# A hybrid decoder step on one core: the order of loads at a stage's start, squares at other tiles, and banks for the last transposes

## The chip, the cores and the metric

The kernel runs on one core of a Trainium2 chip. TensorE does the matrix products, VectorE and ScalarE the work on single elements, GpSimd some of it and the issue of part of the DMAs, and SyncE issues the rest of the DMAs. All run at once and wait for each other by semaphores. The metric is the device time of one execution in microseconds (us), the median of several runs.

## The reference

One layer of a decoder for 512 prompt tokens and 8 single sample tokens, all in float32. D is 2048.

```python
m = mixer(rmsnorm(x, norm_mix_g), ...)   # proj = xn @ w_in; bg, cg, hin, q, k, v, og, glr = split(proj)
#   ya = bg * causal_conv3(cg * hin)                               1024 channels
#   o  = gated linear attention over q, k, v (4 heads), normalised
#   yb = o * silu(og)                                              1024 channels
#   m  = concat(ya, yb) @ w_out
x = x + m
f = conv_ffn(rmsnorm(x, norm_ffn_g), ...)  # h = silu(causal_conv3(u) + b) * v; f = h @ w_down
x = x + f
return rmsnorm(x, final_norm_g), and the new convolution and attention states
```

## The kernel before, in words

Activations lie with channels on the 128 partitions and the 520 tokens along the free axis. Each float32 product is made of three products of parts: an operand is split into a high part (a rounded copy, made by ScalarE, line 111, 123 or 1223) and a low part (the rest, made by VectorE, line 112, 124 or 1227).

**Start (lines 283 to 535).** x comes in rows of tokens and is transposed on TensorE, tile by tile of 128 channels (`x_copy`, copied out of PSUM by VectorE at line 385), scaled and split (`x_split`, low part at line 127), and also stored to memory by a DMA that GpSimd issues (line 389). The loop over k from 0 to 15 multiplies tile k at once by the first weights (line 480, helper line 140), copies up to tile k + 3 and splits tile k + 2. Beside that the squares of x are summed for the norm: ScalarE squares the channels of chunks 1 to 3, and for chunk 0, kept as four tiles of 128x512, GpSimd squares one whole tile in place in each of the iterations k = 8 to 11 (line 492); VectorE sums them at k = 14 and 15. Each of TensorE, VectorE, ScalarE and GpSimd keeps the order in which the program text is written here (`InOrder`, lines 58 to 90).

**Attention and convolution (to line 1122).** The mixer's first projections, the attention of four heads, which leaves its output in memory (`o_d`, line 1093, issued by GpSimd for the last head), and the sums and differences of blocks of x (`mixer_sums`), which go to memory as `mt_d`.

**Mix groups (from line 1640).** The other projections are made with seven products in place of eight: blocks of weights and blocks of x are added first, and each "form" of x is a sum. Form 5 is used by the second product of a group, form 4 by the third, form 6 and 7 later. Form 5, 4 and 6 have three tiles each to fetch from `mt_d` and form 7 four (`load_sum`, line 1599: a DMA on SyncE's queue now, and a function that splits the tile later). Ahead of the loop over `order` (line 1699) the program finishes two tiles of the gate `og`: `y8` and `y9`, each the product of a plain projection, are evacuated (`evac`, line 544), passed through silu, and multiplied by the attention's output `on[0]`, `on[1]`, which is loaded from `o_d` (line 1652). `prepare(i)` (line 1208) makes the high and low part of product i's weights and the next sum of weights. `load_rest(0)` (line 1206) loads a weight block into a buffer that VectorE must have left. From line 823 to line 1799 all five queues, SyncE's and GpSimd's too, keep the order of the text. So in SyncE's queue the loads from `o_d` stand first, then the weight block, then the sums; and on VectorE the product of `y8` with `on[0]` (line 1664, helper 1291) stands between the evacuation of `y8` and the splits.

**The end (lines 1822 to 1903).** The last products of the output are made for two halves of the tokens (`half`): first 264 tokens in three tiles, then 256 in two. For each of 16 tiles m of channels, TensorE multiplies, VectorE adds what was summed before (line 642), and `rows(m)` transposes the result back to rows of tokens (line 1836), one iteration later. Four tiles m share one PSUM bank per tile of tokens. ScalarE squares and sums a bank (line 1846); the last bank in two pieces, columns 0 to 383 after m = 14 and the rest after m = 15. Then come the norm's factor (lines 1880 to 1884, `newton`) and the scaling of four quarters: the first and second by ScalarE (line 1896), the last by VectorE straight out of PSUM (line 1890), the third by VectorE (line 1894), each followed by the store of its result on SyncE's queue (line 1898). Here the framework chooses the order on the engines.

Of the kernel before, what the change touches and what calls it, by code (L numbers as in the profile page):

```python
# [9 lines left out]
F32 = mybir.dt.float32  # L10
# [3 lines left out]
ALU = mybir.AluOpType  # L14
# [3 lines left out]
P = 128  # L18
# [19 lines left out]
def trunk_kernel(  # L38
# [53 lines left out]
    def tmp():  # L92
        return tp.tile([P, T], F32, tag="t", name="t")
# [189 lines left out]
    with ExitStack() as es:  # L283
# [193 lines left out]
        for k in range(KD):  # L477
            c, t = k // 4, k % 4
            for i, ps in enumerate(first if k else ()):
                span(ps, ws[c], xa, k, 4 * (c - i), 1, KD)  # L480
            while upto < min(k + (3 if k < 3 else 4), KD):
                x_copy(upto)
                upto += 1
            if k + 2 < KD:
                x_split(k + 2)
            if t == 0 and c < 2:
                raws.append(load_w(c + 2))
                load_x(xc[c + 2], (c + 2) * 512)
            if t == 1 and c < 3:
                ws.append(parts(raws[c + 1], 8))  # L490
            if 8 <= k < 12:
                nc.gpsimd.tensor_tensor(xc[0][t], xc[0][t], xc[0][t], op=ALU.mult)
# [797 lines left out]
    def mult(out, x, y):  # L1290
        nc.vector.tensor_tensor(out, x, y, op=ALU.mult)
# [355 lines left out]
    w11, first = raw_tile(lambda m, k: mix_source(0, m, k), 1)  # L1647
    nc.sync.dma_start(*first)
    early = {(1, 1): w11, **second_half(lambda m, k: mix_source(0, m, k))}
    on = [tmp()[:, :T] for _ in range(2)]  # L1650
    for j, x in enumerate(on):
        nc.sync.dma_start(x, o_d[j])
    ps = new_mm()
    span(ps, ws_og[0], xa, 0, 0, 8, KD)
    ws = [parts(*raws[0])]
# [166 lines left out]
    def half(b, tiles):  # L1822
        t0, n = PARTS[b]
        fin = fp.tile([P, len(tiles), D], F32, name=f"y{b}")
        sums = fp.tile([P, 3, 5], F32, tag="sums", name="sums", bufs=2)
        nc.vector.memset(sums, 1.0)
        pt, outs = [None], {}

        def rows(m):


            if m % 4 == 0:
                pt[0] = [bank() for _ in tiles]
            out = outs.pop(m)
            for i, (u0, un) in enumerate(tiles):
                nc.tensor.transpose(  # L1836
                    pt[0][i][:un, (m % 4) * P : (m % 4 + 1) * P],
                    out[:, u0 - t0 : u0 - t0 + un], idn,
                )
            if m % 4 == 3 or m == KD - 2:  # L1840
                b = m // 4
                c0, c1 = (0, 512) if b < 3 else ((0, 384), (384, 512))[m % 2]
                for i, (u0, un) in enumerate(tiles):
                    junk = tmp()
                    n = b + (c0 > 0)
                    nc.scalar.activation(
                        junk[:un, c0:c1], pt[0][i][:un, c0:c1], AF.Square,
                        accum_out=sums[:un, i, n : n + 1],
                    )
                    if b < 3:  # L1850
                        f = fin[:un, i, b * 512 : (b + 1) * 512]
                        mult(f, pt[0][i][:un, :], gf[:un, b * 512 : (b + 1) * 512])

        for m2 in range(0, KD, 2):
            wh, wl = piece(w_down, NF - CH, CH, m2 * P, 2 * P)
            for m in (m2, m2 + 1):
                ps = mm_bank()
                co = (m - m2) * P
                for i in range(CH):
                    mm3(  # L1860
                        [ps[:, :n]], (wh[:, i, co : co + P], wl[:, i, co : co + P]),
                        hs[b][i], i == 0, i == CH - 1,
                    )
                    if i == 1:
                        tick()
                outs[m] = tmp()
                q = 2 * (m % 4 // 2)
                for u0, u1 in ((t0, min(t0 + n, HT)), (HT, t0 + n)):
                    if u0 < u1:
                        a = two(acc[m // 4, q + (u0 >= HT)])[:, m % 2, u0 % HT :][:, : u1 - u0]  # L1870
                        add(outs[m][:, u0 - t0 : u1 - t0], ps[:, u0 - t0 : u1 - t0], a)
                if m:
                    rows(m - 1)

        def finish():
# [4 lines left out]
            nc.vector.reduce_sum(var, sums, axis=mybir.AxisListType.X)  # L1880
            nc.scalar.activation(rs, var, AF.Ln, scale=1.0 / D, bias=eps_t)
            nc.vector.tensor_scalar(vv, var, 1.0 / D, EPS, op0=ALU.mult, op1=ALU.add)
            nc.scalar.activation(rs, rs, AF.Exp, scale=-0.5)
            newton(rs, vv, tn, nc.vector)
            for b in (0, 3, 1, 2):
                for i, (u0, un) in enumerate(tiles):
                    f = fin[:un, i, b * 512 : (b + 1) * 512]
                    r = rs[:un, i : i + 1]
                    if b == 3:
                        nc.vector.scalar_tensor_tensor(  # L1890
                            f, pt[0][i][:un, :], r, gf[:un, b * 512 :], op0=ALU.mult, op1=ALU.mult
                        )
# [5 lines left out]
                    nc.sync.dma_start(dst[:, b * 512 : (b + 1) * 512], f)  # L1898

        return finish  # L1900
# [42 lines left out]
```

## Time and profile before

| what | us |
|---|---|
| median of 3 runs | 2163.0 (2161.82 to 2163.73) |
| the profiled execution | 2160.99 |
| its span, first to last instruction | 2159.3 |
| TensorE busy / VectorE / ScalarE / GpSimd | 2134.2 / 1734.5 / 1111.6 / 439.7 |
| stretch 0 to 56 (start), TensorE busy | 53.47 |
| stretch 431 to 477.5 (start of the mix groups), TensorE busy | 43.69 of 46.5 |
| stretch 692 to 840 (output projection and what follows), TensorE busy | 142.12 of 148 |
| stretch 2145.1 to 2159.3 (the end), TensorE busy | 2.56 of 14.2 |

A row of the timeline gives the start in us from the span's start, the duration in us, the engine (PE is TensorE, DVE VectorE, ACT ScalarE, POOL GpSimd, SPq SyncE's queue), the line, the operation, and output<-inputs by the program's names; x2 says that two in a row are merged. A bracket gives the idle time of the engine ahead of the instruction and what ended it. In a row of the grouped waits stand the engine, who was waited for, the time in all, how often, and the longest.

### The profile page before, as it was taken

To read this page: it belongs to the slowest core of one execution; us is meant where nothing else is said; L and a number is where in the kernel's file an instruction comes from. 1 tells how busy PE (TensorE), PEld (TensorE's weight loads), DVE (VectorE), ACT (ScalarE), POOL (GpSimd) and SP (SyncE) were. 2 spreads that over 40 slices of the span, in tenths; PEclk is the share of its full clock that TensorE was granted. 3 is DMA by queue.
4 is the path that set the end of the run, shared out by engine and by line. 5 is a ranking of instruction groups with operands and counts; after the bars stand their busy time and mean duration, and the time that the engine had idled before them with its cause. 6 is when DMAs were issued, how large, how long until landed. Compare 5 with 4: busy or idle time off the path is not lost.

```text
span 2159.3 us, 43820 instructions
## 1 busy us (share of the span) xinstructions
PE 2134.2 (99%) x17749; PEld 2112.2 (98%) x17749; DVE 1734.5 (80%) x2302; ACT 1111.6 (51%) x1631; POOL 439.7 (20%) x625
## 2 busy tenths in 40 slices
PE   9999999999999999999999999999999999999997
PEld 8999999999999999999999999999999999999997
DVE  7347465588888898998998998998998778888886
ACT  6435435355544586555555555555555554444445
POOL 5113131211243421121221131122121300200000
PEclk9999999999999999999999999999999999999999
DMA  8545464388888996667676676676677866994734
GB/s 258 145 131 157 121 190 121 93 247 215 206 259 248 297 268 181 181 183 189 166 191 176 167 195 179 163 198 178 169 193 192 287 206 161 274 291 134 225 108 158
DMA packets 467163, 415.51 MB, mean 192 GB/s; under 512 B 21641, under 2 KB 426393, under 8 KB 466817
## 3 DMA queue, kind: packets, MB, share of 16 engines
q1 hardware_dynamic: 424081, 289.71, 47.0%
q0 software_dynamic: 42832, 122.93, 21.7%
q8 instruction: 139, 2.28, 0.4%
q14 instruction: 63, 0.52, 0.1%
q10 hardware_dynamic: 48, 0.07, 0.0%
HBM read 299.45 MB, written 80.31 MB: 176 GB/s over the span
## 4 chain that ended last, share of the span: by engine, by line
PE 90%; DMA 3%; DVE 3%; ACT 1%; issue 1%; POOL 0%; SPq 0%; ACTq 0%; DVEq 0%; POOLq 0%
PE mm L1247 34%; PE mm L140 14%; PE ms L1247 14%; PE x L1490 9%; PE y L1490 9%; PE f L1490 3%; PE e L1490 3%; PE ms L982 1%; DMA form<-g_d 1%; DMA g_d<-t 1%; DMA yl<-t_d 0%; DMA yl<-mt_d 0%; PE ms L1836 0%; DMA raw<-raw 0%; PE ms L968 0%
## 5 line engine op out<-in xcount | busy, mean ns | idle before, releaser
L1247 PE MATMUL mm<-yl,hi 128*128 128x260 f32 x1696 | 476.6, 281 | 3.4 <-DVE yl L124 3.4
L1247 PE MATMUL mm<-yh,hi 128*128 128x260 f32 x1696 | 476.1, 281 | 2.4 <-ACT ms L1257 1.2
L1247 PE MATMUL mm<-yh,lo 128*128 128x260 f32 x1696 | 475.2, 280 | 0.8 <-DVE lo L1227 0.8
L1223 ACT ACTIVATE hi<-raw 128x1024 fp32r<-128x1024 f32 x324 | 342.0, 1056 | 233.8 <-issue 89.4
L1227 DVE TENSOR_TENSOR lo<-raw,hi 128x1024 fp32r<-128x1024 f32 x324 | 395.4, 1220 | 36.0 <-ACT hi L1223 33.0
L1227 DVE TENSOR_TENSOR lo<-s,hi 128x1024 fp32r<-128x1024 f32 x243 | 298.4, 1228 | 124.9 <-ACT hi L1223 124.9
L1223 ACT ACTIVATE hi<-s 128x1024 fp32r<-128x1024 f32 x243 | 257.4, 1059 | 220.7 <-PE ms L1247 93.6
L1247 PEld LDWEIGHTS mm<-yl,hi 128*128 128x128 f32 x1696 | 319.8, 189 | 4.0 <-DVE yl L124 4.0
L1247 PEld LDWEIGHTS mm<-yh,hi 128*128 128x128 f32 x1696 | 319.5, 188 | 3.0 <-ACT ms L1257 1.4
L1247 PEld LDWEIGHTS mm<-yh,lo 128*128 128x128 f32 x1696 | 319.2, 188 | 1.2 <-DVE lo L1227 1.2
L1247 PE MATMUL ms<-b,hi 128*128 128x260 f32 x1408 | 266.3, 280 | 0.0
L1247 PEld LDWEIGHTS ms<-b,hi 128*128 128x128 f32 x1408 | 223.2, 189 | 0.0
L1490 PE MATMUL x<-form,hi 128*128 128x260 f32 x1120 | 211.5, 281 | 0.1
L1490 PE MATMUL y<-form,hi 128*128 128x260 f32 x1120 | 211.3, 281 | 0.0
L1168 DVE TENSOR_TENSOR s<-s,raw 128x1024 f32<-128x1024 f32 x162 | 197.9, 1221 | 2.8
L1247 PE MATMUL ms<-b,lo 128*128 128x260 f32 x704 | 198.1, 281 | 0.0
L1490 PEld LDWEIGHTS x<-form,hi 128*128 128x128 f32 x1120 | 176.4, 188 | 0.7 <-issue 0.5
L1490 PEld LDWEIGHTS y<-form,hi 128*128 128x128 f32 x1120 | 176.4, 188 | 0.3
L112 DVE TENSOR_TENSOR lo<-raw,hi 128x1024 fp32r<-128x1024 f32 x76 | 94.9, 1253 | 78.0 <-ACT hi L111 77.9
L1490 PE MATMUL x<-form,lo 128*128 128x260 f32 x560 | 156.7, 280 | 0.1
L1490 PE MATMUL y<-form,lo 128*128 128x260 f32 x560 | 156.7, 280 | 0.0
L1247 PEld LDWEIGHTS ms<-b,lo 128*128 128x128 f32 x704 | 132.4, 188 | 0.0
(382 smaller groups left out, 5066.2 us busy)
## 6 DMA issues: line engine op xcount, KB each, us to landing
raw<-in_w_up_dram SPq DMA_DIRECT2D x176, 512.0 KB, 4.6
raw<-in_w_down_dram SPq DMA_DIRECT2D x96, 512.0 KB, 4.7
raw<-in_w_in_dram SPq DMA_DIRECT2D x92, 512.0 KB, 4.5
form<-f_d SPq DMA_DIRECT2D x126, 260.0 KB, 6.2
raw<-raw POOLq DMA_DIRECT2D x56, 512.0 KB, 5.9
f_d<-t POOLq DMA_DIRECT2D x80, 260.0 KB, 5.6
raw<-in_w_out_dram SPq DMA_DIRECT2D x32, 512.0 KB, 13.8
form<-g_d POOLq DMA_DIRECT2D x42, 260.0 KB, 7.6
```

What stands on the lines that cost most here:

```text
L112: nc.vector.tensor_tensor(lo, raw, hi.bitcast(F32), op=ALU.subtract)
L140: nc.tensor.matmul(o, w, xx, start=first and i == 0, stop=last and i == 2)
L982: nc.tensor.matmul(pb[:, c * 64 : (c + 1) * 64], L[:, c, :], rhs[:, c], start=True, stop=True,)
L1168: return lambda: nc.vector.tensor_tensor(out, x, y, op=ALU.add)
L1223: nc.scalar.activation(his[i], src, AF.Copy)
L1227: nc.vector.tensor_tensor(los[i], src, his[i].bitcast(F32), op=ALU.subtract)
L1247: nc.tensor.matmul(st["bank"][b], w[:, k, :], x, start=b not in st["used"] and k == 0 and j == 0, stop=k == 7 and j == 2, skip_group_check ...
L1490: nc.tensor.matmul(ps[:, m, :], w[:, k, m * P : (m + 1) * P], x, start=b not in st["used"] and k == 0 and j == 0, stop=k == 3 and j == 2, ...
```

## The change

There are three edits.

First, at the start of the mix groups: the three loads of the sums of form 5 are issued where the two loads of the attention's output stood, ahead of the weight block. Behind the weight block come the sums of form 4, then the attention's output, then the sums of form 6. The product of `y8` with `on[0]` moves on VectorE from behind the silu to behind the evacuation of `y9`.

Second, in the start: GpSimd squares the four tiles of chunk 0 in iterations 6, 7, 10 and 11 in place of 8, 9, 10 and 11.

Third, at the end: in the half with two tiles of tokens, the transposes of the last tile (m = 15) go to two banks of their own. In both halves the last 512 columns are squared in three pieces (0 to 255 after m = 13, 256 to 383 after m = 14, 384 to 511 after m = 15), with a column more in the table of sums, and where the banks differ the scaling of the last quarter is two instructions.

```diff
-            if 8 <= k < 12:
-                nc.gpsimd.tensor_tensor(xc[0][t], xc[0][t], xc[0][t], op=ALU.mult)
+            if k in (6, 7, 10, 11):
+                x = xc[0][(6, 7, 10, 11).index(k)]
+                nc.gpsimd.tensor_tensor(x, x, x, op=ALU.mult)
...
-    on = [tmp()[:, :T] for _ in range(2)]
-    for j, x in enumerate(on):
-        nc.sync.dma_start(x, o_d[j])
+    put = [load_sum(mt_d, 5, g) for g in range(1, 4)]
     ps = new_mm()
     span(ps, ws_og[0], xa, 0, 0, 8, KD)
     ws = [parts(*raws[0])]
...
     begin(0)
     load_rest(0)
-    put = [load_sum(mt_d, f, g) for f in (5, 4, 6) for g in range(1, 4)]
+    put += [load_sum(mt_d, 4, g) for g in range(1, 4)]
+    on = [tmp()[:, :T] for _ in range(2)]
+    for j, x in enumerate(on):
+        nc.sync.dma_start(x, o_d[j])
+    put += [load_sum(mt_d, 6, g) for g in range(1, 4)]
     y8, y9 = zpad[0][:, 2 : 2 + T], tmp()[:, :T]
     evac(ps, y8)
     nc.scalar.activation(y8, y8, AF.Silu)
-    mult(y8, y8, on[0])
...
     evac(ps, y9)
+    mult(y8, y8, on[0])
     mult(R2, R, R)
...
-        sums = fp.tile([P, 3, 5], F32, tag="sums", name="sums", bufs=2)
+        sums = fp.tile([P, 3, 6], F32, tag="sums", name="sums", bufs=2)
...
+            if m == KD - 1:
+                pt[1] = [bank() for _ in tiles] if len(tiles) < 3 else pt[0]
+            pb = pt[m == KD - 1]
...
-            if m % 4 == 3 or m == KD - 2:
+            if m % 4 == 3 or m > KD - 4:
                 b = m // 4
-                c0, c1 = (0, 512) if b < 3 else ((0, 384), (384, 512))[m % 2]
+                c0, c1 = (0, 512) if b < 3 else ((0, 256), (256, 384), (384, 512))[m - 13]
...
                     if b == 3:
-                        nc.vector.scalar_tensor_tensor(
-                            f, pt[0][i][:un, :], r, gf[:un, b * 512 :], op0=ALU.mult, op1=ALU.mult
-                        )
+                        cuts = (0, 512) if pt[1] is pt[0] else (0, 384, 512)
+                        for pb, c0, c1 in zip(pt, cuts, cuts[1:]):
+                            nc.vector.scalar_tensor_tensor(
+                                f[:, c0:c1], pb[i][:un, c0:c1], r, gf[:un, b * 512 + c0 : b * 512 + c1],
+                                op0=ALU.mult, op1=ALU.mult,
+                            )
```

More of the change, by code (lines that the diff above doesn't have):

```diff
@@ L1824, in half @@
         fin = fp.tile([P, len(tiles), D], F32, name=f"y{b}")
-        sums = fp.tile([P, 3, 5], F32, tag="sums", name="sums", bufs=2)
+        sums = fp.tile([P, 3, 6], F32, tag="sums", name="sums", bufs=2)
         nc.vector.memset(sums, 1.0)
-        pt, outs = [None], {}
+        pt, outs = [None, None], {}
         def rows(m):
@@ L1836, in rows @@
                 nc.tensor.transpose(
[L1837 removed]
+                    pb[i][:un, (m % 4) * P : (m % 4 + 1) * P],
                     out[:, u0 - t0 : u0 - t0 + un], idn,
                 )
[L1840 removed]
+            if m % 4 == 3 or m > KD - 4:
                 b = m // 4
[L1842 removed]
+                c0, c1 = (0, 512) if b < 3 else ((0, 256), (256, 384), (384, 512))[m - 13]
                 for i, (u0, un) in enumerate(tiles):
                     junk = tmp()
[L1845 removed]
+                    n = b + (m - 13 if b == 3 else 0)
                     nc.scalar.activation(
[L1847 removed]
+                        junk[:un, c0:c1], pb[i][:un, c0:c1], AF.Square,
                         accum_out=sums[:un, i, n : n + 1],
```

## The prediction

> **What bounds the kernel now.** I read the page first, then the busy time of each engine by stretch, then TensorE's waits in the stretches that the change touches.
>
> ```profile
> PE 2134.2 (99%) x17749; PEld 2112.2 (98%) x17749; DVE 1734.5 (80%) x2302; ACT 1111.6 (51%) x1631; POOL 439.7 (20%) x625
> ```
>
> TensorE is busy for 2134.2 of 2159.3 us. The change touches no matmul of the large products, so it can only win back idle time of TensorE, 25.1 us in all, and only where it acts: in the first 56 us, at the start of the mix groups, and behind the last product. By stretch (columns: length, then busy time and instructions of TensorE, its weight loads, VectorE, ScalarE, GpSimd, the granted clock, DMA share, GB/s):
>
> ```profile
> 431.00:477.50 46.50, 43.69 (x358) 42.69 (x357) 36.77 (x57) 22.78 (x34) 7.62 (x12) 1.00 0.89 255
> 477.50:692.00 214.50, 214.48 (x1805) 214.49 (x1806) 187.56 (x232) 110.83 (x156) 65.28 (x91) 1.00 0.82 228
> 2145.10:2159.30 14.20, 2.56 (x19) 1.94 (x17) 4.04 (x12) 4.80 (x14) 0.00 (x0) 0.73 0.40 148
> ```
>
> At the start of the mix groups 46.50 - 43.69 = 2.8 us of TensorE are idle, and in the 214 us behind it nothing is. So what TensorE gains there isn't lost again directly. The end is a serial chain of 14.2 us. The timeline names the waits that the change is near (the bracket is the idle time ahead of the instruction and who ended it):
>
> ```profile
> 38.12 0.51 PE L140 MATMUL mm<-xl,hi 128*128 128x260 f32 x2 [0.61 <-DVE xl L127]
> 463.24 0.39 PE L1247 MATMUL mm<-yh,hi 128*128 128x260 f32 x1 [1.24 <-ACT ms L1257]
> 464.04 0.39 PE L1247 MATMUL mm<-yh,lo 128*128 128x260 f32 x1 [0.41 <-DVE lo L1227]
> 471.02 0.39 PE L1247 MATMUL mm<-yh,lo 128*128 128x260 f32 x1 [0.39 <-DVE lo L1227]
> 477.52 0.36 PE L1247 MATMUL mm<-yh,hi 128*128 128x260 f32 x1 [0.66 <-DVE t L642]
> 2147.57 0.80 PE L1836 MATMUL ms<-idn,t 128*128 128x128 f32 x2 [0.56 <-ACT t L1846]
> ```
>
> The ceiling is then 0.61 in the start, 1.24 + 0.41 + 0.39 + 0.66 = 2.7 in mix, and about 0.6 at the end: 3.9 us, or 0.18%. A measurement of this kernel can tell about 0.2% (4.3 us) from no change.
>
> **Part one: sums of x ahead of the attention's output.** The loads of SyncE's queue in the order of the kernel before:
>
> ```profile
> 437.56 2.87 SPq L1652 DMA_DIRECT2D t<-o_d  x2
> 440.86 0.38 SPq L1206 DMA_DIRECT2D raw<-in_w_in_dram  x1
> 441.30 16.04 SPq L1603 DMA_DIRECT2D yl<-mt_d  x13
> ```
>
> The thirteen loads of sums (form 5, form 4, form 6, three each, then form 7) stand behind the two loads of the attention's output and a weight load that is let go at 440.86 only. Among the waits of that queue (us in all, times, longest) is one that tells when a load lands:
>
> ```profile
> SPq L1603 <- DMA t<-o_d: 3.4, 2, 2.9
> ```
>
> Two issues of sums waited for the loads from o_d, which they have no data in common with. These are the ninth and the tenth load from the first of o_d on. So eight are in flight at most, and an issue that waits shows when the load eight places ahead has landed:
>
> ```profile
> 448.85 0.32 SPq L1603 DMA_DIRECT2D yl<-mt_d  x1
> 452.04 0.32 SPq L1603 DMA_DIRECT2D yl<-mt_d  x1
> 453.58 0.32 SPq L1603 DMA_DIRECT2D yl<-mt_d  x1
> 456.30 0.32 SPq L1603 DMA_DIRECT2D yl<-mt_d  x1
> 457.01 0.32 SPq L1603 DMA_DIRECT2D yl<-mt_d  x1
> ```
>
> In order these are the landings of the first o_d load, the second, the weights, and (the three of form 5 being between) the first and second sum of form 4. The first sum of form 5 lands when ScalarE starts to split it, at 454.32 below. What VectorE does with that:
>
> ```profile
> 448.88 0.70 DVE L1291 TENSOR_TENSOR zpad<-zpad,t 128x520 f32<-128x520 f32 x1 [3.62 <-DMA t<-o_d]
> 454.99 2.00 DVE L124 TENSOR_TENSOR yl<-yl,yh 128x520 fp32r<-128x520 f32 x3 [3.14 <-ACT yh L123]
> 461.48 0.76 DVE L544 TENSOR_TENSOR t<-mm,R 128x260 f32<-128x260 f32 x2
> 454.32 1.94 ACT L123 ACTIVATE yh<-yl 128x520 fp32r<-128x520 f32 x3 [7.44 <-DMA yl<-mt_d]
> 456.17 1.05 ACT L1223 ACTIVATE hi<-s 128x1024 fp32r<-128x1024 f32 x1
> 457.25 1.23 DVE L1227 TENSOR_TENSOR lo<-s,hi 128x1024 fp32r<-128x1024 f32 x1 [0.25 <-ACT hi L1223]
> ```
>
> VectorE idles 3.62 us for the attention's output and 3.14 us for the sums; of its 9.7 us of idle time in the stretch (46.50 - 36.77) these are 6.8, and behind 454.99 it is nearly full. TensorE's four waits are that lateness: the evacuation at 461.48 gates ScalarE's silu and the copy behind it (463.24), the others name VectorE.
>
> With the change the sums of form 5 take the places of the two o_d loads and half the place of the weights. By bytes (260 KB a sum, 512 KB the weights) they land at 448.85, 452.04 and (452.04 + 453.58)/2 = 452.8; the weights at 454.3, the sums of form 4 by 456.3, the first o_d load at 457.0. The DMA engines move no byte less, so the gain is one of order alone. VectorE's chain: third sum 452.8, its high part 0.6 (a third of 1.94), high part of the weight sum 1.05, low part 1.23, the next weight sum as long as that, 1.2, three low parts of form 4 2.0: 458.9 in place of 461.48 for the evacuation, 2.6 us earlier, or 2.9 if low parts and evacuation follow each other with the overlap of the pipeline, as the rows there do. Then comes the product with the attention's output, 0.7, which before was done at 448.88 and now stands here, so all behind it is 1.9 to 2.2 us earlier. TensorE has 2.7 us to win, VectorE's lead allows 2.2: I take **2.2**. Ends: 1.2 if the third sum lands with the whole of the weights' place lost (453.6 to 453.8), 2.7 if VectorE's lead is larger than TensorE's idle time. The moved product waits for a load that lands at 457.0 and is asked for at 459.4; behind it queue the square of R, the next low part and the second gate's product, so 2.4 us of cover stand there. The sums of forms 6 and 7 keep their place in bytes and cost nothing; the weights land 0.7 later, for the fourth product.
>
> **Part two: squares at other tiles.** GpSimd squares four tiles of 128x512. What they do to VectorE:
>
> ```profile
> 31.80 1.05 POOL L492 TENSOR_TENSOR x<-x 128x512 f32<-128x512 f32 x1
> 34.65 1.06 POOL L492 TENSOR_TENSOR x<-x 128x512 f32<-128x512 f32 x1
> 31.50 1.65 DVE L298 TENSOR_TENSOR wg<-wgraw,wg 128x256 fp32r<-128x256 f32 x1
> 33.07 0.68 DVE L385 COPY t<-tp 128x520 f32<-128x520 f32 x1
> 34.35 2.44 DVE L112 TENSOR_TENSOR lo<-raw,hi 128x1024 fp32r<-128x1024 f32 x1
> 24.96 1.22 DVE L112 TENSOR_TENSOR lo<-raw,hi 128x1024 fp32r<-128x1024 f32 x1
> 26.70 0.75 DVE L127 SCALAR_TENSOR_TENSOR xl<-t,gm,xh 128x520 fp32r<-128x520 f32 x1
> 28.46 0.40 PE L140 MATMUL mm<-xl,hi 128*128 128x260 f32 x2
> ```
>
> The same low part takes 1.22 alone and 2.44 beside a square: VectorE stood for the square's 1.05 us and a little more. The third and fourth square stay where they are, so the stretched low part at 34.35, from which the wait at 38.12 comes, stays stretched. The second square leaves 31.80, and the small subtraction there (1.65) loses about 1.05. The copy behind it (33.07) waits for transposes too, so not all of that comes through: between 0 and 1.05 I put it at 0.4 to 0.5, and the wait of 0.61 shrinks to 0.1 or 0.2. Against that the first square, now behind the DMA of tile 8, falls at about 25.1, on the low part at 24.96: if that becomes 2.44, the low part of tile 8 ends at 26.70 + 1.2 + 0.75 = 28.65, and TensorE, which reads it at 28.46, waits 0.2 to 0.3. Net **0.25** (0.61 - 0.25 - 0.1); if the first square waits instead, 0.5; ends 0 and 0.6.
>
> The Trainium skill, SBUF — State Buffer, section Who interferes with whom, says that a VectorE instruction with two SBUF inputs and a GpSimd instruction that reads SBUF contend, and that issue order decides who blocks. By that rule the low part at 24.96 would go first and the square would wait: 0.5 here, and 3.2 in the sum below instead of 2.95. The trace differs as far as it can show starts: at 31.50 and 34.35 VectorE's record begins 0.30 us ahead of the square's and VectorE is still the one that is stretched.
>
> **Part three: the last tile's transposes in banks of their own.**
>
> ```profile
> 2146.83 0.42 DVE L642 TENSOR_TENSOR t<-mm,acc 128x256 f32<-128x256 f32 x1 [1.22 <-PE mm L140]
> 2146.94 0.49 ACT L1846 ACTIVATE t<-ms 128x384 f32<-128x384 f32 x1 [3.65 <-PE ms L1836]
> 2147.94 0.28 ACT L1846 ACTIVATE t<-ms 128x128 f32<-128x128 f32 x1
> 2148.41 0.28 ACT L1846 ACTIVATE t<-ms 128x128 f32<-128x128 f32 x1
> 2148.81 0.17 DVE L1880 TENSOR_REDUCE fin<-sums 128x3 f32<-128x15 f32 x1 [1.56 <-ACT t L1846]
> 2151.12 4.45 SPq L1898 DMA_DIRECT2D out_dram<-y  x8
> ```
>
> The last sum is ready at 2147.25; the transposes start at 2147.57 since ScalarE still squares 384 columns of the same bank, and the second follows the second square. With banks of their own they start at about 2147.3, both. ScalarE has done columns 0 to 255 in its 3.65 us of idle time, and its squares of 128 columns for tile 14 end at about 2147.5. The first last square starts 0.37 behind the transposes as before (2147.94 - 2147.57): 2147.67. The second is 0.25 to 0.36 behind it, and the reduction 0.40 behind that (2148.81 - 2148.41): 2148.3 to 2148.4, in place of 2148.81. Gain **0.5**, with ends 0.4 and 0.6. The product of the last quarter is cut in two, four VectorE instructions for two; but the results leave one by one on SyncE's queue for 4.45 us, of which these are the third and fourth, so some 0.1 us more on each is covered; without the cover it would cost 0.3. In the first half three tiles share their banks still: tile 14's transposes now wait for squares of tile 13. The row of 2147.57 prices such a wait at 0.56; three of them would be 1.7. I take 0: a tile's twelve matmuls lie between, and a square of 256 columns is shorter than the 0.49 of 384.
>
> **The sum**: 2.2 + 0.25 + 0.5 = 2.95 us. The profiled run took 2160.99 us, 1.7 more than its span and 2.0 less than the median of the three timed (2163.0, 2161.82 to 2163.73). From the median: **2160.0 us**, 0.14% less.
>
> **Rivals.** (1) The whole of it: VectorE's lead covers all of TensorE's 2.7 us, the square waits for VectorE, and the end gives 0.6: 3.8 to 3.9, with up to 0.2 from squares of 128 columns in place of 384 between the halves: 4.0 us, 2159.0. For it: the landings are inferred from the bytes, and a third sum 0.6 us earlier is enough. Against: VectorE is nearly full from 454.99 on, and has the extra 0.7. (2) The order of loads wins little: the sums wait for something that the queue's order doesn't show (the memory of their tiles), or land with the weights; mix gives 0 to 0.8, all together 1.2: 2161.8. Against: the first sums were issued as soon as the queue was free. (3) Slower, by one wait that takes the place of the one removed: VectorE at the product with the attention's output. It decides from 459.4 on, and each microsecond later is one of TensorE; beyond 462.4 the kernel is slower than before. The price if that load, let go at about 452.04, takes as long as the weight load of 440.86 did:
>
> ```profile
> raw<-in_w_in_dram SPq DMA_DIRECT2D x1, 512.0 KB, 12.7
> ```
>
> It lands at 464.7, 5.3 late: 2163.0 - 2.95 + 5.3 = 2165.4. Against: by its place in bytes it lands at 457.0.
>
> **How the numbers follow.** Forecast 0.52, (1) 0.28, (2) 0.14, (3) 0.06. The three runs of before spread over 1.9 us, so a median is good to some 0.7. Faster by over 0.2%, under 2158.7: half of (1) and one in ten of the forecast, 0.14 + 0.05 = 0.19. Slower by over 0.2%, over 2167.3: half of (3), 0.03. Within: 0.78. The range leaves out (3), half of (2) and a quarter of (1), 0.2 in all: 2158.3 to 2162.0.
>
> **What would show it.** In the changed profile: the loads from mt_d start at about 437.6 on SyncE's queue, ahead of the weight load, and those from o_d behind six of them; ScalarE's first split of a sum at about 449; VectorE's idle stretches of 3.62 and 3.14 gone or moved; the evacuation at about 458.8; TensorE busy for about 45.9 of 46.5 us there; a low part of about 2.4 us near 25 and another near 34; the last transposes with no wait, and the reduction some 1.5 us after the last sum's start in place of 1.98. Wrong would be: an idle stretch of VectorE ahead of the product with the attention's output, or the sums landing at 454 as before.

## The result, and the profile after

| | before | changed |
|---|---|---|
| median, us (15 runs each) | 2162.97 (2160.67 to 2165.12) | 2157.83 (2156.63 to 2160.74) |
| ratio | | 0.9982, 95% interval 0.9975 to 0.9989 |
| profiled execution / its span, us | 2160.99 / 2159.3 | 2159.98 / 2158.2 |

The ratio says 3.9 us less (2.4 to 5.4), within the 0.2% that count as no change here. The two profiled executions lie only 1.0 us apart, and the first rows of TensorE show why they can't be subtracted from each other. These are TensorE's first products of the weights in the kernel before and then in the changed one, at a place that the change does not reach (its first edit acts at tile 6):

```profile
7.97 0.28 PE L460 MATMUL mm<-ch,hi 128*128 128x260 f32 x1
11.17 0.39 PE L140 MATMUL mm<-ch,hi 128*128 128x260 f32 x1
```

```profile
9.66 0.42 PE L460 MATMUL mm<-ch,hi 128*128 128x260 f32 x1
13.18 0.39 PE L140 MATMUL mm<-ch,hi 128*128 128x260 f32 x1
```

The profiled execution of the changed kernel was 2.01 us late before the change could act (the last section says what its trace shows of that). So stages are compared, each from an instruction ahead of it to one behind it. For the mix groups the pair is VectorE's last update of the attention's output, called the anchor below, and a copy of ScalarE out of TensorE's results, 196 us later. Kernel before, then changed:

```profile
432.65 0.75 DVE L1089 SCALAR_TENSOR_TENSOR o<-o,par,t 128x520 f32<-128x520 f32 x1
629.17 0.37 ACT L1257 ACTIVATE ms<-mm 128x260 f32<-128x260 f32 x1
```

```profile
433.86 0.75 DVE L1090 SCALAR_TENSOR_TENSOR o<-o,par,t 128x520 f32<-128x520 f32 x1
628.91 0.37 ACT L1258 ACTIVATE ms<-mm 128x260 f32<-128x260 f32 x1
```

It was 196.52 us and is 195.05: the mix groups gained **1.47 us in this execution**. By stretches (length, TensorE busy, weight loads, VectorE, ScalarE, GpSimd, granted clock, DMA share, GB/s), changed kernel:

```profile
431.00:477.50 46.50, 44.84 (x370) 44.05 (x369) 38.32 (x59) 23.15 (x35) 7.93 (x13) 1.00 0.90 256
477.50:692.00 214.50, 214.50 (x1808) 214.50 (x1808) 187.63 (x233) 110.80 (x157) 65.45 (x91) 1.00 0.82 228
```

What was won ahead of 477.5 isn't lost behind it. The queue of SyncE, the splits of the sums of form 5 on ScalarE, and what comes of them on VectorE and TensorE, in the changed kernel:

```profile
438.73 3.24 SPq L1604 DMA_DIRECT2D yl<-mt_d  x3
442.07 0.59 SPq L1207 DMA_DIRECT2D raw<-in_w_in_dram  x1
442.76 8.14 SPq L1604 DMA_DIRECT2D yl<-mt_d  x3
450.99 1.14 SPq L1662 DMA_DIRECT2D t<-o_d  x2
...
450.33 0.64 ACT L123 ACTIVATE yh<-yl 128x520 fp32r<-128x520 f32 x1 [2.24 <-DMA yl<-mt_d]
453.81 0.64 ACT L123 ACTIVATE yh<-yl 128x520 fp32r<-128x520 f32 x1 [2.84 <-DMA yl<-mt_d]
454.77 0.64 ACT L123 ACTIVATE yh<-yl 128x520 fp32r<-128x520 f32 x1 [0.32 <-DMA yl<-mt_d]
...
460.63 0.76 DVE L545 TENSOR_TENSOR t<-mm,R 128x260 f32<-128x260 f32 x2
461.30 0.69 DVE L1292 TENSOR_TENSOR zpad<-zpad,t 128x520 f32<-128x520 f32 x1
461.91 0.69 DVE L1292 TENSOR_TENSOR R<-R 128x520 f32<-128x520 f32 x1
...
463.79 0.39 PE L1248 MATMUL mm<-yh,lo 128*128 128x260 f32 x1 [0.46 <-DVE lo L1228]
477.28 0.35 PE L1248 MATMUL mm<-yh,hi 128*128 128x260 f32 x1 [0.66 <-DVE t L643]
```

The order is as forecast: six sums and the weights go ahead of the attention's output. VectorE's product (461.30) waits for nothing: by the updates of its semaphore in the trace, the load from o_d landed at 459.23, 2.1 us ahead. But the third sum is split only at 454.77, which is 20.91 us behind the anchor, where by bytes 20.15 was expected (452.8 - 432.65). Of TensorE's four waits the first, 1.24, is gone; 0.46, 0.40 and 0.66 are left.

The start: VectorE's two stretched low parts and the subtraction that is no longer stretched, and GpSimd's first square:

```profile
26.96 2.28 DVE L112 TENSOR_TENSOR lo<-raw,hi 128x1024 fp32r<-128x1024 f32 x1
33.71 0.42 DVE L298 TENSOR_TENSOR wg<-wgraw,wg 128x256 fp32r<-128x256 f32 x1
35.94 2.41 DVE L112 TENSOR_TENSOR lo<-raw,hi 128x1024 fp32r<-128x1024 f32 x1
...
27.09 1.05 POOL L493 TENSOR_TENSOR x<-x 128x512 f32<-128x512 f32 x1
...
56.80 0.39 PE L140 MATMUL mm<-bh,hi 128*128 128x260 f32 x1 [0.58 <-DVE k L545]
```

The last row is the instruction that stood at 55.26 before: 43.62 us behind the first product, where it was 44.09. So the start gained **0.47**. The subtraction takes 0.42 in place of 1.65, and of TensorE's waits in the tile loop none is left that the timeline names.

The end:

```profile
2146.20 0.42 DVE L643 TENSOR_TENSOR t<-mm,acc 128x256 f32<-128x256 f32 x1 [1.22 <-PE mm L140]
2146.68 0.44 PE L1842 MATMUL ms<-idn,t 128*128 128x128 f32 x2 [0.30 <-DVE t L643]
2147.76 0.17 DVE L1886 TENSOR_REDUCE fin<-sums 128x3 f32<-128x18 f32 x1 [1.14 <-ACT t L1852]
2150.07 4.46 SPq L1907 DMA_DIRECT2D out_dram<-y  x8
```

Both last transposes follow the sum at once, none waits for ScalarE, and the reduction starts 1.56 us behind the sum's start, where it was 1.98: **0.42**. The queue of stores is as long as before, so the two added products are covered.

### The profile page after: what moved, and what is told of

The parts are those of the page before. It is cut to its first block, busy times and chain, and to the rows that moved or that the text cites. A ratio compares the mean times of both kernels' runs of the same rounds, so it can differ in the third digit from the quotient of the medians.

```text
span 2158.2 us, 43832 instructions
## 1 busy us (share of the span) xinstructions
PE 2135.7 (99%) x17749; PEld 2114.0 (98%) x17749; DVE 1734.6 (80%) x2304; ACT 1111.9 (52%) x1641; POOL 438.0 (20%) x625
## 3 DMA queue, kind: packets, MB, share of 16 engines
q8 instruction: 139, 2.28, 0.5%
## 4 chain that ended last, share of the span: by engine, by line
PE 87%; DVE 4%; issue 4%; DMA 4%; ACT 1%; POOL 1%; SPq 0%; ACTq 0%; DVEq 0%; POOLq 0%
PE mm L1248 34%; PE ms L1248 14%; PE mm L140 13%; PE x L1491 8%; PE y L1491 8%; PE e L1491 3%; PE f L1491 3%; DVE lo L1228 1%; DMA x_d<-acc 1%; PE ms L983 1%; DVE acc L1510 1%; DMA yl<-mt_d 0%; DMA raw<-raw 0%; PE ms L1842 0%; PE tp L306 0%
```

## The experiments

Theory A, formed on this trace: each part gains what its own stage shows, and the mix groups gain VectorE's lead, which is set by the landing of the third sum. It was set against rivals in each run below. Stage gains are taken from the profiles (to about 0.05 us), times from the ratio to the kernel before.

**The order alone** (kernel before with the first part only):

```diff
-    on = [tmp()[:, :T] for _ in range(2)]
-    for j, x in enumerate(on):
-        nc.sync.dma_start(x, o_d[j])
+    put = [load_sum(mt_d, 5, g) for g in range(1, 4)]
...
```

> Kernel before with the order of the loads alone (sums of form 5 ahead, the loads from o_d behind form 4, the product with the attention's output behind the evacuation of y9). Theory A: the mix groups gain what VectorE's lead leaves after that product, and the lead is set by the landing of the third sum of form 5. Then the TensorE instruction that stood at 477.52 stands 1.45 us earlier measured from an instruction ahead of the stage (the VectorE instruction of 432.65 in the kernel before), the evacuation of y9 at about 459.4 in the clock of the kernel before, and the timed ratio is 0.9993 (1.5 us less). Rival B, the order is worth nothing and the stage's gain came from the earlier start (VectorE ahead of its due time): no gain in the stage, ratio 1.0000. Rival C, the lead is larger without the other parts: 2.2 us or more, ratio 0.9990.

Measured: 0.9989 (0.998 to 0.9998), 2.4 us less. The profile gained far more than 1.45: from the anchor at 432.49 to the copy at 625.19 it takes 192.70 us, a gain of 3.82, and TensorE has no wait in the stretch that the timeline names. This execution was the quickest of its eleven (2157.05, median 2159.48). The splits and VectorE's evacuation in it:

```profile
449.00 0.64 ACT L123 ACTIVATE yh<-yl 128x520 fp32r<-128x520 f32 x1 [1.76 <-DMA g_d<-t]
451.04 0.64 ACT L123 ACTIVATE yh<-yl 128x520 fp32r<-128x520 f32 x1 [1.41 <-DMA yl<-mt_d]
...
456.89 0.76 DVE L544 TENSOR_TENSOR t<-mm,R 128x260 f32<-128x260 f32 x2
```

With the same queue in the same order the third sum is split 18.55 us behind the anchor, and not 20.91. Two things follow: something other than the order sets that time, and 3.82 is more than the 2.7 that the prediction took as all there was.

**The squares alone** (kernel before with the second part only):

```diff
-            if 8 <= k < 12:
+            if k in (6, 7, 10, 11):
...
```

> Kernel before with the squares of x at the other tiles alone. Theory A: TensorE's wait of 0.61 ahead of the instruction at 38.12 goes, since the small subtraction at 31.50 takes 0.42 in place of 1.65; two low parts are stretched to 2.3 to 2.4 (near 25 and near 34); between the first product of the stage and the instruction at 55.26 0.4 to 0.5 us less; nothing changes behind it; ratio 0.9998. Rival B, the squares only move the wait: a wait of 0.3 or more appears near 28.5, the stage gains less than 0.2. Rival C, the early start is worth more later, in the mix groups, since VectorE is ahead: 1 us or more at 477.52, ratio 0.9993.

Measured: 1.0000 (0.9991 to 1.0008), too coarse for 0.4 us. The stage: 55.03 - 11.38 = 43.65, a gain of 0.44; the mix groups take 0.02 more. Theory A holds; the early start is worth nothing more later.

**The banks alone** (two lists of banks in place of one, squares in three pieces):

```diff
-            pt, outs = [None], {}
+            pt, outs = [None, None], {}
+            if m == KD - 1:
+                pt[1] = [bank() for _ in tiles] if len(tiles) < 3 else pt[0]
...
```

> Kernel before with the banks of the last tile's transposes alone. Theory A: the reduction starts 1.14 us behind the end of the last sum in place of 1.56, so 0.4 us at the end; between the halves another 0.2 to 0.4, since the wait for squares of 384 columns is gone; ratio 0.9996 to 0.9997. Rival B, only the end gains: 0.4. Rival C, the two added products at the end are on the path after all: the store queue at the end gets longer than 4.45 us or starts no earlier, gain 0.2 or less.

Measured: 0.9999 (0.999 to 1.0008). In the profile the reduction starts 1.57 us behind the last sum's start (2146.89 - 2145.32), 0.41 gained; from a sum of VectorE ahead of the first half's last tiles (2112.95 in the kernel before) to the last sum it is 0.25 less. So 0.67 from there to the reduction, as theory A said. The transposes of the first half's last tile, in the kernel before and then with these banks, show what went between the halves:

```profile
2121.67 0.33 PE L1836 MATMUL ms<-idn,t 128*128 128x128 f32 x1
2122.18 0.28 PE L1836 MATMUL ms<-idn,t 128*128 128x128 f32 x1
2122.66 0.27 PE L1836 MATMUL ms<-idn,t 128*8 128x128 f32 x1
```

```profile
2119.69 0.49 PE L1839 MATMUL ms<-idn,t 128*128 128x128 f32 x3
```

They started half a microsecond apart, each behind a square of ScalarE (0.47 to 0.48 us for 384 columns) and with products between them, and now follow each other. All nine profiles with these banks show 0.63 to 0.70 here, and the four others without them 0.00 to 0.02.

**The changed kernel again.** Since the order alone had won more in mix than the whole change, both were run again, unaltered. A kernel meant to leave stores out numbered the pairs of tiles wrongly, so that no store was left out; it is a third repetition.

> The changed kernel once more, unaltered, since the order of the loads alone gained more in its profile (all four waits of TensorE in the mix stretch gone, busy for 46.42 of 46.50 us) than the whole change did in its own (44.84 of 46.50). Theory N (the time at which the third sum lands differs from execution to execution, by how the DMA engines serve the stores that are under way): in one of two repetitions at least the third sum lands 1 us or more earlier than in the first profile, and TensorE is busy for 46 us or more; the timed ratio is again near 0.9982, that is 2.7 us from mix and the rest from the other two parts. Rival S (the squares or the banks move tiles in memory and so take back part of what the order wins): both repetitions show the evacuation of y9 26.5 to 27.1 us behind the VectorE instruction of 433.86 of the first profile, and TensorE's waits of 0.46, 0.40 and 0.66.

> The second repetition of the changed kernel; the same expectations as for the first.

> The changed kernel without the stores of the last pair of convolution tiles to g_d (their place is filled with the pair before, stored a second time at its own time; the part of the output that comes from the last pair is then another). Theory W (the stores that GpSimd lets go at 438 to 443 share the DMA engines with the loads and halve their rate from 448 to 454 in the clock of the kernel before): no stretch of 2 us under 300 GB/s between 446 and 458, the third sum of form 5 lands by the queue's bytes at 390 GB/s, 3 us or more earlier than in the first profile of the changed kernel (453.5 in that clock), TensorE idles 0.3 us or less in the mix stretch, and the kernel is 0 to 1.3 us faster than the changed one, less what the second copy of the pair before costs. Rival Q (the rate of the loads is low there by themselves): the dip stays, and the third sum lands at 452 or later.

> The order of the loads alone, once more, unaltered. Its first profile gained 3.82 us in the mix stretch (ScalarE's copies of 620 to 630 us stand 3.82 earlier measured from the VectorE instruction of 432.65), the four profiles of the changed kernel 1.36 to 2.39. Theory N (the landing of the third sum differs by execution): the two repetitions lie in the range 1.3 to 3.9 us and at least one of them under 3.0; the third sum lands where ScalarE's third split begins, 18.5 to 21.0 us behind that VectorE instruction, and the gain follows it. Rival S (the other two parts take some of it back): both repetitions gain 3.5 us or more.

> The second repetition of the order alone; the same expectations as for the first.

| profile | third split, us behind the anchor | evacuation of y9, behind the anchor | gain of mix, us | ratio |
|---|---|---|---|---|
| before | | 28.83 | 0 | |
| squares alone | | 28.86 | -0.02 | 1.0000 (0.9991 to 1.0008) |
| banks alone | | 28.64 | 0.20 | 0.9999 (0.9990 to 1.0008) |
| changed | 20.91 | 26.77 | 1.47 | 0.9982 |
| changed, again | 20.45 | 26.30 | 1.93 | 0.9979 (0.9970 to 0.9988) |
| changed, again | 21.00 | 26.86 | 1.36 | |
| changed (misnumbered) | 19.98 | 25.83 | 2.39 | 0.9975 (0.9966 to 0.9984) |
| order alone | 18.55 | 24.40 | 3.82 | 0.9989 (0.9980 to 0.9998) |
| order alone, again | 20.08 | 25.94 | 2.28 | 0.9986 (0.9977 to 0.9995) |
| order alone, again | 20.31 (second half of a merged row) | 26.17 | 2.05 | |

The squares alone and the banks alone have the old queue, and show that the stage of the kernel before repeats to 0.2 us.

Theory N's spread is there: the order alone gave 2.28 and 2.05 when repeated, inside the 1.36 to 2.39 of the changed kernel, so rival S as it was stated (3.5 or more in both repetitions) falls. That the other parts take back a little isn't excluded: the three profiles of the order alone gain 2.72 on the mean, the four of the changed kernel 1.79. N's stronger guesses, a landing 1 us earlier and 46 us of TensorE in one repetition of the changed kernel, did not come true (0.46 earlier at best in the two, 0.93 in the third; 45.35, 44.77, and 45.47 in the third). What does hold is a rule almost without scatter: gain and split add up to 22.36 to 22.38 in all seven rows with the new queue. From 21.0 down to 18.55 us, each microsecond by which the third sum is split earlier is one of the mix groups.

**The stores out.** What moves the landing? While the sums load, seven stores to g_d that GpSimd let go at 438 to 443 are under way. Here the first pair's tiles are stored twice, at 294 us, and the second pair's not at all, so that part of the output is another:

```diff
-        for d, x in zip(dst, (hi, src)):
+        for d, x in zip(dst, (hi, src) * (len(dst) // 2)):
...
-                stored(src, [dst[f : f + n, x, i] for x in range(2)], tmp())
+                to = {0: (0, 1), 1: ()}.get(i, (i,))
+                stored(src, [dst[f : f + n, x, m] for m in to for x in range(2)], tmp())
```

> The changed kernel without the stores of the second pair of convolution tiles to g_d (the first pair is stored twice, at its own time near 294 us; the part of the output that comes from the second pair is then another). In the kernel tried as no_stores the pairs were numbered wrongly, and it was the changed kernel. Theory W (the stores that GpSimd lets go at 438 to 443 share the DMA engines with the loads and halve the loads' rate from 447 to 453): no stretch of 2 us under 300 GB/s between 446 and 458, the third sum of form 5 lands 18.0 us or less behind the VectorE instruction of 432.65 (20.45 to 21.0 in the changed kernel), and the mix stretch gains 3.3 to 3.9 us on the kernel before. Rival Q (the rate is low there by the loads themselves): the dip stays, the gain is 1.3 to 2.4.

The same four microseconds, first the changed kernel, then without the stores (the last column is GB/s):

```profile
448.00:450.00 2.00, 2.00 (x19) 2.00 (x18) 1.82 (x2) 0.09 (x1) 0.00 (x0) 1.00 1.13 187
450.00:452.00 2.00, 2.00 (x19) 2.00 (x18) 0.70 (x1) 0.64 (x1) 0.00 (x0) 1.00 1.06 227
```

```profile
448.00:450.00 2.00, 2.00 (x19) 2.00 (x18) 1.48 (x2) 2.00 (x5) 0.00 (x0) 1.00 1.06 381
450.00:452.00 2.00, 2.00 (x19) 2.00 (x18) 2.00 (x4) 0.58 (x2) 0.00 (x0) 1.00 1.05 393
```

And from its timeline:

```profile
448.91 1.68 ACT L123 ACTIVATE yh<-yl 128x520 fp32r<-128x520 f32 x3
...
458.10 0.77 DVE L545 TENSOR_TENSOR t<-mm,R 128x260 f32<-128x260 f32 x2 [0.17 <-PE mm L140]
```

Theory W: the engines are as busy (1.13 and 1.06 against 1.06 and 1.05) and move half as much while the stores are among their work. By queue, from 448 to 452 (packets, MB, share of the 16 engines' time; q0 has the stores that GpSimd issues, q1 the loads that SyncE issues), the changed kernel and then without the stores:

```profile
q0 software_dynamic: 165, 0.54, 59.4%
q1 hardware_dynamic: 319, 0.29, 50.4%
```

```profile
q1 hardware_dynamic: 874, 1.55, 105.4%
```

The stores take more than half of the engines' time, and the loads move 0.29 MB in place of 1.55. Without the stores ScalarE never waits for a sum of form 5: its three splits stand back to back, the third 15.2 us behind the anchor (which is at 434.77), TensorE has no wait at all and the mix groups gain 4.13, more than the 3.9 expected. Two stretches are under 300 GB/s against the expectation, though not by stores: behind 452 (275) and 456 (289), at shares of 0.87 and 0.88; ahead of 452.46 an issue of SyncE's queue waited 2.0 us for TensorE. The time is 0.9974 (0.9964 to 0.9984). The Trainium skill, DMA: Bandwidth & Descriptors, section Issuing engines are not separate DMA queues, says that transfers of all issuing engines run on the same 16 DMA engines and interleave; these rows agree.

Two things limit this. The halved total is not what stores always do: from 444 to 448 in the changed kernel they have 55 and 65% of the engines' time, and 338 and 375 GB/s are moved; why the total falls behind 448 is open. And without the stores other waits go too: in five of the seven profiles of the table the row of the second split names a store as what it waited for, and not its load. That does not decide here, since by the semaphores the second sum landed within 0.12 us of that moment, and the third split waits for its own load in six of the seven (in the merged row it follows the second). Whether the landing still scatters without the stores is not shown, with one profile.

**Parts first, and both ahead.** If the wait for the sums can't be removed, VectorE can work in it. In the first kernel the low part of the second weight set stands ahead of the splits of form 5; in the second the load of the rest of the weights also goes behind form 4:

```diff
     prepare(0)
-    for x in put[:3]:
-        x()
     span(ps, ws[1], xa, 8, 8, 8, KD)
     prepare(1)
-    for x in put[3:6]:
+    for x in put[:6]:
         x()
```

> The changed kernel with the low part of the second weight set ahead of the splits of form 5 on ScalarE and VectorE, the queue as in the changed kernel. Theory A (VectorE idles while the sums land, and the second low part behind them is on the path): VectorE does the low part and the sum of the third set, 2.4 us, in that idle time, so the evacuation follows the third sum's landing by 2.4 us less (in the first profile of the changed kernel it came 6.9 us behind it: here 4.5 or less, and no wait of TensorE in the stretch but the 0.66, whenever the sums land). Against the changed kernel 0 to 1.2 us, by how late the sums land there. Rival B: the weights' high part or the fourth product waits in its place, and the evacuation comes no earlier.

> The changed kernel with the low part of the second weight set ahead of the splits of form 5 on ScalarE and VectorE, and the load of the rest of the weights behind form 4 and the loads from o_d. Theory A (the third sum of form 5 gates ScalarE's second high part, and with it VectorE's second low part): the second low part stands in VectorE's idle time while the sums land, the sums land some 0.7 to 1.5 earlier, the evacuation of y9 comes at 457.6 or earlier in the clock of the kernel before (459.4 in the changed kernel), TensorE is busy for 46.1 or more of 46.5 us in the stretch, and the kernel is 1.0 to 1.3 us faster than the changed one: ratio to the kernel before 0.9976 to 0.9978. Rival B, the bytes decide and the wait only moves: the weights that now land later hold TensorE at the fourth product, or VectorE waits for the loads from o_d at the product; evacuation earlier, but the instruction at 477.52 no earlier than in the changed kernel, ratio 0.9982. Rival C, it is slower than the changed kernel since the late rest of the weights stalls the third low part: ratio over 0.9985.

Parts first, VectorE and TensorE:

```profile
450.74 1.23 DVE L1228 TENSOR_TENSOR lo<-s,hi 128x1024 fp32r<-128x1024 f32 x1 [2.87 <-ACT hi L1224]
453.14 3.86 DVE L124 TENSOR_TENSOR yl<-yl,yh 128x520 fp32r<-128x520 f32 x6
456.91 0.76 DVE L545 TENSOR_TENSOR t<-mm,R 128x260 f32<-128x260 f32 x2
...
473.56 0.36 PE L1248 MATMUL mm<-yh,hi 128*128 128x260 f32 x1 [0.66 <-DVE t L643]
```

The low part that stood behind the third sum stands ahead of all six splits now. The evacuation comes 25.01 us behind the anchor (at 431.90), mix gains 3.21, and 0.66 is the only wait that the timeline names. Both ahead: 24.90, gain 3.33, and a wait of 0.57; TensorE was busy for 45.93 us of the stretch, where 46.1 was expected. In these two and in the seven profiles of the table VectorE's lead at the evacuation (28.83 less its place there), less the 0.61 us that the moved product takes (461.30 to 461.91), is the gain to 0.02 us: 28.83 - 24.90 - 0.61 = 3.32.

So theory A holds in kind, but the new place of the low part is worth less than the 2.4 us that it said. By the semaphores the third sum landed 19.66 us behind the anchor in parts first and 20.19 in both ahead. By the rule of the table such landings give 2.7 and 2.2 anyway, so 0.5 and 1.2 us are the new order's, in one execution each. The evacuation follows the landing by 5.3 and 4.7 us, against 5.9 in the changed kernel (26.77 - 20.91; the expectation took 6.9), and 4.5 or less was expected for parts first. What is late next is form 4: in parts first ScalarE's second three splits wait 1.97 us for it, at 454.25. In both ahead it landed 1.5 us earlier behind the anchor (20.81 against 22.32), with the weight load moved behind it. The times, 0.9976 (0.9967 to 0.9985) and 0.9980 (0.9971 to 0.9989), can't be told from the changed kernel's own; the profiles are ahead of it by 0.8 to 2.0 us in this stretch.

**The product in place.** The changed kernel with `mult(y8, y8, on[0])` back ahead of the first low part:

```diff
     nc.scalar.activation(y8, y8, AF.Silu)
+    mult(y8, y8, on[0])
...
     evac(ps, y9)
-    mult(y8, y8, on[0])
```

> The changed kernel with the product with the attention's output back at its old place, ahead of the first low part, while its load stays behind form 4. All theories of the queue: VectorE stands at that product until the load lands, at 458 in the clock of the kernel before (25 us behind the VectorE instruction of 432.65), and the first low part of the second gate's weights, for which TensorE waits at 450 in that clock, comes 1.9 us later: TensorE idles some 9 to 11 us there, and the kernel takes 8 to 10 us more than the kernel before, about 2170. If the load does not decide (it lands when asked, whatever stands ahead in the queue): no such stall.

```profile
455.05 0.28 PE L1248 MATMUL mm<-bh,hi 128*128 128x260 f32 x1
...
457.16 0.70 DVE L1292 TENSOR_TENSOR zpad<-zpad,t 128x520 f32<-128x520 f32 x1 [12.74 <-DMA t<-o_d]
...
460.18 0.59 PE L1248 MATMUL mm<-bh,lo 128*128 128x260 f32 x1 [4.84 <-DVE lo L1228]
```

Its busy times right behind that wait:

```profile
460.10:464.40 4.30, 4.22 (x19) 4.22 (x20) 4.27 (x7) 1.66 (x4) 0.00 (x0) 0.50 1.12 300
```

The queue decides: the load lands 25.35 us behind the anchor (25 expected), VectorE stands for 12.74 us, and the mix groups take 5.46 us more than in the kernel before; the single execution took 2163.95 beside a median of 2161.77. My expectation was too dark (8 to 10): it took the low part that waits for one that TensorE needs at 450, and TensorE needs it only behind 455.05. The last row shows what else a long wait costs: the granted clock is 0.50 for the 4.3 us behind it (19 matmuls where 36 would fit at 0.12 us). The Trainium skill, TensorE: Matmul & The Clock Gate, section Part 1, says that the clock falls to half after an idle window of about 3.4 us and comes back after as long a busy one. The trace agrees in kind: its clock records have half speed from 458.08 (2.75 us into the wait, a little sooner than a whole window) to 464.91, 4.7 us after TensorE is busy again.

## Why the prediction was right, and where it was not

*The forecast.* No measurable change, 0.14% faster, was right as a class: 0.18% (0.11 to 0.25) was measured. The median, 2157.83, lies 0.5 us below the range; the ratio applied to the 2163.0 of the prediction gives 2159.1, inside it, and as near to rival (1) as numbers can be.

*Part one, the order: right, with the mechanism in each step.* Sums first, the weights and form 4 behind them, the product with no wait, the evacuation earlier, and the gain equal to VectorE's lead less the product. Over the seven profiles of this queue the third sum is split 20.18 us behind the anchor on the mean (20.15 from the bytes), the evacuation comes at 26.04 (458.8 was 26.15), and the gain is 2.19 (2.2). One sign was missed: TensorE was to be busy for about 45.9 of 46.5 us, and it was for 44.84, 45.35, 44.77 and 45.47 in the four profiles of the changed kernel; busy time rises by less than the gain, 1.15 for 1.47 in the first, by what the next paragraph says of brackets. The agreement of means is partly luck: one execution gives 1.36 and another 3.82, and the prediction gave no cause for a spread. The rate that it took from the bytes is a mean over a stretch in which stores and loads interleave.

*The ceiling: wrong.* "TensorE has 2.7 us to win" added up the idle times in brackets. These are not what a wait costs. The kernel before, ahead of the first wait (463.24, bracket 1.24), and a stall without a bracket:

```profile
461.60 0.28 PE L1247 MATMUL mm<-yh,lo 128*128 128x260 f32 x1
461.72 0.28 PE L1247 MATMUL mm<-yl,hi 128*128 128x260 f32 x1
...
467.12 0.28 PE L1247 MATMUL ms<-xh,hi 128*128 128x260 f32 x1
467.53 0.39 PE L1247 MATMUL ms<-xh,lo 128*128 128x260 f32 x1
467.75 0.28 PE L1247 MATMUL ms<-xl,hi 128*128 128x260 f32 x1
```

Running, matmuls start 0.12 us apart, though each record is 0.28 long; the bracket counts from the record's end. From 461.72 to 463.24 it is 1.52, so this wait cost 1.40. The stall at 467.53 (0.41 from the start before it, and 0.22 behind) costs 0.39; it begins only 0.13 behind the end of a record, and has no bracket. Counted so, with the step behind each, the other three cost 0.78, 0.65 and 0.90, and the stretch held 4.1 us, not 2.7. This is why the order alone could win 3.82, with no wait named by the timeline, and the kernel without the stores 4.13, which is all of it. In every profile what is left by this count is 4.1 less the gain, to 0.1 us. The end of the range for this term, 2.7, was too low.

*Part two, the squares: the right direction, 0.25 forecast and 0.44 to 0.47 measured.* Both stretched low parts are there. The failed step is the wait of 0.2 to 0.3 for the low part of tile 8: it was ready at 30.51, or 28.50 in the clock of the kernel before, and not at 28.65, and TensorE, which had read it at 28.46, read it 0.1 later. GpSimd's record starts 0.13 behind VectorE's and VectorE is still the one stretched, 2.28 in place of 1.22. By the rule of the Trainium skill that was cited (SBUF — State Buffer, Who interferes with whom) the square would have waited; as far as the records' starts tell who came first, the trace decides against it here.

*Part three, the banks: 0.42 at the end where 0.5 was forecast, and 0.25 between the halves where 0 was taken.* The prediction's own rows gave 0.38 to 0.49 for the end (2148.81 less 2148.32 to 2148.43), so 0.5 was its upper edge. The waits of tile 14 for squares of tile 13 cost nothing that the timeline names, as argued. What was left out is that the change also cuts the squares of 384 columns for which tile 15's transposes in the first half waited; only rival (1) had this, at up to 0.2.

*The rivals.* (1) gave the number, but not for its reasons: the square doesn't wait for VectorE, and the lead in the changed kernel's four profiles does not cover TensorE's whole stall. (2) is out: the least gain of the order is 1.36. (3) didn't occur, but the product in place shows that its mechanism is real, and, in one profile, that the change gains only with the product moved.

*What stays open.* The stages sum to 1.36 to 2.39 + 0.46 + 0.67, 2.5 to 3.5 us, and the three measurements of the changed kernel give 3.9, 4.5 and 5.4, each good to 1.5 to 2 us. The profiles can't decide whether there is more: the stretch from the copy at 629 to the last reduction, which no part but the banks' 0.67 touches, takes 1517.9 to 1521.1 us in fourteen profiles without order by kernel.

## What to carry to other kernels

Price a TensorE wait from the start of the matmul before it to the start of the one behind it, less one step of the running pipeline; the idle time in brackets leaves out what the overlapping records hide. When a load that gates the path shares the DMA engines with stores, its landing is a spread and not a number (2.5 us here): put work that needs no load ahead of the instructions that wait for it, and move what does need the later load behind them. For gains under the noise of the whole, compare the same stage in several profiles, each from an instruction ahead of it.

## What the runs showed of the hardware that was not expected

- With stores and loads under way together from 448 to 452, the DMA engines moved half at equal busy share: 187 and 227 GB/s against 381 and 393 without the stores. From 444 to 448 the same mix moved 338 and 375. The landing of one load some 20 us behind the anchor scattered over 2.5 us (18.55 to 21.00) between executions of one order.
- Four of fourteen profiles, the changed kernel's among them, start 2 us later: their first matmuls of 128x260 take 0.42 us in place of 0.28. The column of the granted clock shows 1.00 there in both, but only because the trace has no clock record that early. Its first records are the rise to full speed, at 10.06 to 10.38 us in these four and at 4.11 to 5.85 in the other ten; in the changed kernel's profile the matmuls go from 0.41 to 0.28 between 10.10 and 10.46, and 0.42 is also what they take at the granted clock of 0.50 in the product in place. So these starts ran at a lower clock for longer. Why it rose late is open; the change is not the cause, since its repetitions have one of each.
- A wait of 4.84 us of TensorE was followed by 4.3 us at a granted clock of 0.50.
- In all the profiles with the squares at their new places a square of GpSimd that starts 0.13 to 0.14 us behind VectorE's low part stretches it from 1.22 to 2.28 or 2.29 us.
